# First mixer of a two-layer decoder trunk: narrow matmuls that add up in PSUM, an earlier softmax, and row sums from a token-major copy of x

## The chip, the cores and the metric

One Trainium2 chip; the kernel runs on 1 of its cores. The metric is device time in microseconds (us), the median of several runs; a profile is one execution seen by the hardware profiler.

## The reference

Two pre-norm residual layers on x of 256 tokens by 2048 channels, float32. The change touches the first layer's mixer only:

```python
h = rmsnorm(x, norm_mix[0])
u = h @ w_in                      # q, k, v (8 heads x 128), a, gate (1024 each)
q = partial_rope(q) * HEAD_DIM ** -0.5;  k = partial_rope(k)
y_a = dilated_attention(q, k, v)  # three causal windows, merged by their softmax sums
g = a * sigmoid(gate)
g = causal_dwconv(g, conv_w) + conv_b            # width 31
y_b = silu(layernorm(g))
x = x + concat([y_a, y_b]) @ w_out
```

After it come a gated FFN with a width-3 convolution, a second layer (forgetting attention and the same FFN), and a last norm.

## The kernel before, in words

Activations stand channel-major: `xT` holds 16 tiles of 128 channels by 256 tokens. Every operand of a large matmul is split in two parts, high and low: x into `xs` (L183 to L187: ACT makes the high part, DVE the low part), each piece of weights into `whi` (a cast on ACT, L95) and `wlo` (a subtraction on DVE, L96). `stream` (L79) loads weights through three raw buffers, all DMAs of it on SP's queue, splits them into four buffers of each part, and yields 2 row tiles at a time.

`panel_b` (L100) makes 512 output channels as four PSUM tiles (five exist). For each tile `m` and row tile `k` there are two matmuls: the high weights against both parts of x at once, 512 columns (L109), into the two halves of the tile, and the low weights against the high part of x, 256 columns (L110), into the left half. So the left half and the right half must be added when the tile is read: `whole` (L113) copies the right half on ACT and adds on DVE; `add_x` (L202) adds both halves to x on DVE. `panel_a` (L126), for v, has the tokens on the partitions and three matmuls of 512 columns.

The first mixer (L261 to L455) runs these panels in turn: four gate panels `ag0` to `ag3` (two tiles of a and two of gate each), `q0`, `q1`, `k0`, `k1`, the value panels `v0`, `v1`, the output projection of the attention half `oa0` to `oa3` (8 row tiles each), then of the convolution half `ob0` to `ob3`. The first norm's scale is applied after the projection, as `rb`. Its sum of squares comes from `square_x` (L189): ACT squares each tile of x, POOL adds (L195), four matmuls against ones (L179) sum over channels. `softmax_t` (L217) makes the scores of 4 heads (PE, L225), mask and maximum (DVE, L229), exponentials (ACT, L235), the scaling (ACT, L241), transposes (PE, L246) and copies back (ACT, L247); `weigh_v` (L250) multiplies with v. The convolution's 31 taps run on DVE and ACT beside all this, from a list that `fill_in` (L71) empties at a pace; after `oa1` the layer norm follows (L417): column sums (L425), the mean off (L432), squares, their sums (L434), a matmul (L179), the inverse root, its broadcast by a matmul (`bc_ln`, L169), then for each of 8 channel tiles a product (L437), Silu (L438), and the split into high (L439) and low (L440). `ob0` needs these.

A scheduler orders each engine's instructions by priorities and estimated times: `tc.high_priority(offset=n)` lets a block go ahead, `tc.issue_after` holds a DMA until another one is issued. The order is fixed at build time; each engine then works through its own list.

Of the kernel before, what the change touches and what calls it, by code (L numbers as in the profile page):

```python
# [41 lines left out]
def trunk(ctx, tc, a):  # L42
# [56 lines left out]

    def panel_b(src_of, x2, kts, name, order=(0, 1, 2, 3), dk=4):  # L100


        acc = {m: pacc.tile([P, 512], F32, tag="acc", name=f"acc_{name}_{m}") for m in order}
        for ks, hi, lo in stream(src_of, len(kts), P * len(order), name, dk):
            for m in order:
                ms = slice(m * P, (m + 1) * P)
                for j, k in enumerate(ks):
                    x = x2(kts[k])
                    PE.matmul(acc[m], hi[:, j, ms], x.rearrange("p a t -> p (a t)"), start=k == 0, stop=False)  # L109
                    PE.matmul(acc[m][:, :T], lo[:, j, ms], x[:, 0, :], start=False, stop=k == len(kts) - 1)  # L110
        return acc
# [51 lines left out]
    def along_free(r, name):  # L163
# [8 lines left out]
        return rb  # L172

    def rstd_from(parts, n, name):
# [5 lines left out]
        r = rsqrt_cols(ps[:, 0:2], 1.0 / n, name)  # L180
        return r, along_free(r, name)

# [6 lines left out]
    def square_x(kt, ssq, name):  # L189
        if kt == 0:  # L190
            S.activation(ssq, xT[:, kt, :], AF.Square)
        else:
            sq = wk.tile([P, T], F32, tag="sq", name=f"sq_{name}_{kt}")
            S.activation(sq, xT[:, kt, :], AF.Square)
            (G if name == "m0" else V).tensor_tensor(out=ssq, in0=ssq, in1=sq, op=ALU.add)  # L195

# [64 lines left out]
    with ExitStack() as ph:  # L261
# [121 lines left out]
        def qk_panel(c0, r, name):  # L383
            acc = panel_b(cols(w_in, c0 // 512), x2, list(range(KT)), name)
# [281 lines left out]
def _laid_out(inputs):  # L666
# [57 lines left out]
```

## Time and profile before

| | us |
|---|---|
| median of 3 runs | 2268.2 (2265.68 to 2268.28) |
| the profiled execution's own time | 2266.76 |
| its span, first to last instruction | 2265.0 |
| PE busy in the span | 2226.5 |
| DVE busy in the span | 1510.7 |
| ACT busy in the span | 1131.3 |

The profiled execution is 1.4 us under the median, and 1.8 us of it lie outside the span. Matmuls are pipelined and their ends are modelled, so PE's progress is read from the starts of its instructions and from its waits, not from its busy time.

### The profile page before, as it was taken

To read this page: it belongs to the slowest core of one execution; us is meant where nothing else is said; L and a number is where in the kernel's file an instruction comes from. 1 tells how busy PE (TensorE), PEld (TensorE's weight loads), DVE (VectorE), ACT (ScalarE), POOL (GpSimd) and SP (SyncE) were. 2 spreads that over 40 slices of the span, in tenths; PEclk is the share of its full clock that TensorE was granted. 3 is DMA by queue.
4 is the path that set the end of the run, shared out by engine and by line. 5 is a ranking of instruction groups with operands and counts; after the bars stand their busy time and mean duration, and the time that the engine had idled before them with its cause. 6 is when DMAs were issued, how large, how long until landed. Compare 5 with 4: busy or idle time off the path is not lost.

```text
span 2265.0 us, 30815 instructions
## 1 busy us (share of the span) xinstructions
PE 2226.5 (98%) x12142; PEld 1915.6 (85%) x12142; DVE 1510.7 (67%) x2307; ACT 1131.3 (50%) x1619; POOL 45.5 (2%) x77
## 2 busy tenths in 40 slices
PE   8999889999999999999999999999999999999997
PEld 7888778888888888888888888888888888888886
DVE  6999988776754576666655555666766644676644
ACT  6667655454443344444554444555444433444433
POOL 2000000000000000000010000000000000000001
PEclk9999899999999999999999999999999999999999
DMA  7554345555555545555545444555455555545453
GB/s 254 186 183 171 129 151 186 186 186 187 186 186 194 189 176 204 185 187 186 190 151 186 166 152 165 186 186 203 177 191 192 187 187 194 193 172 203 168 190 126
DMA packets 60225, 411.90 MB, mean 182 GB/s; under 512 B 7232, under 2 KB 7936, under 8 KB 11696
## 3 DMA queue, kind: packets, MB, share of 16 engines
q1 hardware_dynamic: 59328, 408.62, 50.7%
q8 instruction: 95, 1.56, 0.3%
q10 hardware_dynamic: 144, 1.05, 0.1%
q14 instruction: 50, 0.41, 0.1%
q0 software_dynamic: 608, 0.26, 0.0%
HBM read 407.75 MB, written 2.10 MB: 181 GB/s over the span
## 4 chain that ended last, share of the span: by engine, by line
PE 97%; DVE 1%; ACT 1%; DMA 0%; issue 0%; SPq 0%; ACTq 0%; DVEq 0%
PE acc_g L109 15%; PE acc_u L109 14%; PE acc_g L110 7%; PE acc_u L110 7%; PE acc_d L109 7%; PE acc_q L109 4%; PE acc_k L109 4%; PE acc_d L110 4%; PE acc_oc L109 3%; PE acc_ag L109 2%; PE acc_q L110 2%; PE acc_k L110 2%; PE acc_v L122 2%; PE acc_v L123 2%; PE acc_d L122 2%; PE acc_d L124 2%
## 5 line engine op out<-in xcount | busy, mean ns | idle before, releaser
L109 PE MATMUL acc_g<-xs,whi_g 128*128 128x512 f32 x1408 | 493.1, 397 | 0.0
L109 PE MATMUL acc_u<-xs,whi_u 128*128 128x512 f32 x1408 | 481.9, 395 | 0.0
L110 PE MATMUL acc_g<-xs,wlo_g 128*128 128x256 f32 x1408 | 388.8, 280 | 0.0
L110 PE MATMUL acc_u<-xs,wlo_u 128*128 128x256 f32 x1408 | 370.0, 279 | 0.0
L96 DVE TENSOR_TENSOR wlo_g<-raw_g,whi_g 128x1024 fp32r<-128x1024 f32 x176 | 215.1, 1223 | 166.2 <-ACT whi_g L95 166.2
L109 PEld LDWEIGHTS acc_g<-xs,whi_g 128*128 128x128 f32 x1408 | 262.6, 188 | 60.7
L95 ACT CAST whi_u<-raw_u 128x1024 fp32r<-128x1024 f32 x176 | 185.1, 1052 | 239.9 <-PE acc_u L109 122.0
L109 PEld LDWEIGHTS acc_u<-xs,whi_u 128*128 128x128 f32 x1408 | 260.1, 188 | 52.7
L96 DVE TENSOR_TENSOR wlo_u<-raw_u,whi_u 128x1024 fp32r<-128x1024 f32 x176 | 213.1, 1221 | 116.6 <-ACT whi_u L95 116.6
L95 ACT CAST whi_g<-raw_g 128x1024 fp32r<-128x1024 f32 x176 | 184.9, 1051 | 198.1 <-PE acc_u L109 91.3
L96 DVE TENSOR_TENSOR wlo_d<-raw_d,whi_d 128x1024 fp32r<-128x1024 f32 x136 | 166.5, 1224 | 161.5 <-ACT whi_d L95 161.3
L110 PEld LDWEIGHTS acc_u<-xs,wlo_u 128*128 128x128 f32 x1408 | 265.0, 188 | 9.0
L110 PEld LDWEIGHTS acc_g<-xs,wlo_g 128*128 128x128 f32 x1408 | 265.6, 189 | 3.0 <-DVE wlo_g L96 0.2
L95 ACT CAST whi_d<-raw_d 128x1024 fp32r<-128x1024 f32 x136 | 143.0, 1051 | 207.2 <-PE acc_d L109 118.9
L109 PE MATMUL acc_d<-hp,whi_d 128*128 128x512 f32 x704 | 245.2, 394 | 0.0
L110 PE MATMUL acc_d<-hp,wlo_d 128*128 128x256 f32 x704 | 194.4, 283 | 0.0
L109 PEld LDWEIGHTS acc_d<-hp,whi_d 128*128 128x128 f32 x704 | 131.3, 188 | 28.8
L110 PEld LDWEIGHTS acc_d<-hp,wlo_d 128*128 128x128 f32 x704 | 132.3, 188 | 1.9
L109 PE MATMUL acc_q<-xs,whi_q 128*128 128x512 f32 x384 | 133.8, 396 | 0.0
L109 PE MATMUL acc_k<-xs,whi_k 128*128 128x512 f32 x384 | 131.7, 394 | 0.0
L110 PE MATMUL acc_q<-xs,wlo_q 128*128 128x256 f32 x384 | 104.5, 282 | 0.0
L110 PE MATMUL acc_k<-xs,wlo_k 128*128 128x256 f32 x384 | 102.0, 279 | 0.0
(296 smaller groups left out, 3858.4 us busy)
## 6 DMA issues: line engine op xcount, KB each, us to landing
raw_g<-in_ffn_w_up SPq DMA_DIRECT2D x88, 1024.0 KB, 4.8
raw_u<-in_ffn_w_up SPq DMA_DIRECT2D x88, 1024.0 KB, 4.8
raw_d<-in_ffn_w_down SPq DMA_DIRECT2D x68, 1024.0 KB, 4.8
raw_q<-in_od_w_in SPq DMA_DIRECT2D x16, 1024.0 KB, 4.8
raw_k<-in_od_w_in SPq DMA_DIRECT2D x16, 1024.0 KB, 4.8
raw_v<-in_od_w_in SPq DMA_DIRECT2D x16, 1024.0 KB, 4.8
raw_oc<-in_od_w_out SPq DMA_DIRECT2D x16, 1024.0 KB, 4.8
raw_e<-in_ffn_w_down SPq DMA_DIRECT2D x16, 1024.0 KB, 4.7
```

What stands on the lines that cost most here:

```text
L95: S.copy(hi, rv[:, h:h + half, :])
L96: last = V.tensor_tensor(out=lo, in0=rv[:, h:h + half, :], in1=hi.bitcast(F32), op=ALU.subtract)
L109: PE.matmul(acc[m], hi[:, j, ms], x.rearrange("p a t -> p (a t)"), start=k == 0, stop=False)
L110: PE.matmul(acc[m][:, :T], lo[:, j, ms], x[:, 0, :], start=False, stop=k == len(kts) - 1)
L122: PE.matmul(o, xh, hi, start=first, stop=False)
L123: PE.matmul(o, xh, lo, start=False, stop=False)
L124: PE.matmul(o, xl, hi, start=False, stop=last)
```

## The change

It does five things in the first mixer, and nothing elsewhere.

1. `panel_b` gets `wide=False` for `ag`, `q`, `k` and `oa`: the 512-column matmul becomes two of 256 columns with the same weights, one for each part of x, both into the left half of the PSUM tile. All products then add up in PSUM.
2. Readers of these tiles take one half: `whole` goes, the q and k panels multiply by the norm's scale straight from PSUM, `add_x` makes one addition instead of two, and `ag_glu` is rewritten.
3. The first norm's sums: x is loaded a second time, token-major, in four pieces of 128 by 1024; ACT squares each with an accumulated row sum, DVE adds two sums per token. The sixteen squares, POOL's additions and four matmuls go.
4. `softmax_t` of the first mixer is traced with `high_priority(offset=200)`.
5. A host-side copy of x in the inputs (`x_tok`), and a function split in two (`rstd_of`).

```diff
-    def panel_b(src_of, x2, kts, name, order=(0, 1, 2, 3), dk=4):
+    def panel_b(src_of, x2, kts, name, order=(0, 1, 2, 3), dk=4, wide=True):
...
-                    PE.matmul(acc[m], hi[:, j, ms], x.rearrange("p a t -> p (a t)"), start=k == 0, stop=False)
+                    if wide:
+                        PE.matmul(acc[m], hi[:, j, ms], x.rearrange("p a t -> p (a t)"), start=k == 0, stop=False)
+                    else:
+                        PE.matmul(acc[m][:, :T], hi[:, j, ms], x[:, 0, :], start=k == 0, stop=False)
+                        PE.matmul(acc[m][:, :T], hi[:, j, ms], x[:, 1, :], start=False, stop=False)
...
-    def add_x(acc, i, then=None):
+    def add_x(acc, i, then=None, wide=True):
...
-            V.tensor_tensor(out=x, in0=acc[m][:, T:], in1=x, op=ALU.add)
+            if wide:
+                V.tensor_tensor(out=x, in0=acc[m][:, T:], in1=x, op=ALU.add)
             V.tensor_tensor(out=x, in0=acc[m][:, :T], in1=x, op=ALU.add)
...
-                for kt in range(c, c + n):
-                    square_x(kt, ssq0, "m0")
...
             for j in range(2):
-                whole(sg[:, j, :], acc[2 + j], f"g{i}{j}")
+                V.tensor_tensor(out=sg[:, j, :], in0=acc[2 + j][:, :T], in1=rb, op=ALU.mult)
+            S.activation(sg, sg, AF.Sigmoid)
+            V.tensor_tensor(out=sg, in0=sg, in1=rb.unsqueeze(1).broadcast_to([P, 2, T]), op=ALU.mult)
             for j in range(2):
-                whole(ab[:, j, :], acc[j], f"a{i}{j}")
-            V.tensor_tensor(out=sg, in0=sg, in1=rb2, op=ALU.mult)
-            S.activation(sg, sg, AF.Sigmoid)
-            V.tensor_tensor(out=sg, in0=sg, in1=rb2, op=ALU.mult)
-            V.tensor_tensor(out=ab, in0=ab, in1=sg, op=ALU.mult)
+                V.tensor_tensor(out=glu[:, 2 * i + j, KW - 1:], in0=acc[j][:, :T], in1=sg[:, j, :], op=ALU.mult)
...
+        with tc.high_priority(offset=400):
+            for i in range(4):
+                t, h = divmod(i, 2)
+                xtok = x0.tile([P, 1024], F32, name=f"xtok{i}", tag="xtok", bufs=2)
+                with tc.issue_after(loads[4].ins):
+                    nc.sync.dma_start(out=xtok, in_=a["x_tok"][t * P:(t + 1) * P, 1024 * h:1024 * (h + 1)])
+                S.activation(xtok, xtok, AF.Square, accum_out=sq0[:, i:i + 1])
+            V.reduce_sum(out=ss0, in_=sq0.rearrange("p (t h) -> p t h", t=2), axis=AX.X)
...
             for m in range(4):
-                whole(full[:, m, :], acc[m], f"{name}{m}")
-            V.tensor_tensor(out=full, in0=full, in1=r.unsqueeze(1).broadcast_to([P, 4, T]), op=ALU.mult)
+                V.tensor_tensor(out=full[:, m, :], in0=acc[m][:, :T], in1=r, op=ALU.mult)
...
-            pts.append(softmax_t(mx, qf[hg], kf, mask, f"e{hg}", act_scale=True))
+            with tc.high_priority(offset=200):
+                pts.append(softmax_t(mx, qf[hg], kf, mask, f"e{hg}", act_scale=True))
```

From the first matmul of `ob0` on, PE's and DVE's lists are the same in both kernels. Ahead of it the scheduler places many things anew. Three places follow. The lines of the changed kernel are its own: L113 and L114 are the two narrow matmuls, L115 the low weights' (L110 before), L255 the transposes (L246), L348 the new loads, L282 the loads of x (L274).

SP's queue in the first gate panel, before (L86 loads weights, L336 and L337 constants):

```order
L86 DMA raw_ag_6_192<-in_ev_w_in 128x1024
L86 DMA raw_ag_8_224<-in_ev_w_in 128x1024
L86 DMA raw_ag_10_257<-in_ev_w_in 128x1024
L86 DMA raw_ag_12_290<-in_ev_w_in 128x1024
L86 DMA raw_ag_14_322<-in_ev_w_in 128x1024
L336 DMA cst<-in_c_ident 128x130
L337 DMA cw<-in_ev_conv_w 128x248
L86 DMA raw_ag_0_399<-in_ev_w_in 128x2048
L86 DMA raw_ag_4_448<-in_ev_w_in 128x2048
```

and now:

```order
L86 DMA raw_ag_6_199<-in_ev_w_in 128x1024
L86 DMA raw_ag_8_233<-in_ev_w_in 128x1024
L348 DMA xtok_375<-in_x_tok 128x1024
L348 DMA xtok_378<-in_x_tok 128x1024
L86 DMA raw_ag_10_268<-in_ev_w_in 128x1024
L86 DMA raw_ag_12_303<-in_ev_w_in 128x1024
L86 DMA raw_ag_14_337<-in_ev_w_in 128x1024
L348 DMA xtok_381<-in_x_tok 128x1024
L341 DMA cst<-in_c_ident 128x130
L342 DMA cw<-in_ev_conv_w 128x248
L348 DMA xtok_384<-in_x_tok 128x1024
L86 DMA raw_ag_0_418<-in_ev_w_in 128x2048
```

Two of the new loads stand ahead of the panel's sixth piece of weights, two ahead of the next panel's first.

PE at the end of the second value panel, before: the transposes of the second softmax (`tp_e_2121` and on) stand behind the panel's last matmuls.

```order
L122 MATMUL acc_v_1_2341<-whi_v_14_2487,xs 128x512
L123 MATMUL acc_v_1_2341<-wlo_v_14_2488,xs 128x512
L124 MATMUL acc_v_1_2341<-whi_v_14_2487,xs 128x512
L246 MATMUL tp_e_2121<-cst,pt_e_2085 128x128 x3
L246 MATMUL tp_e_2128<-cst,pt_e_2086 128x128 x3
L246 MATMUL tp_e_2135<-cst,pt_e_2087 128x128 x3
L246 MATMUL tp_e_2142<-cst,pt_e_2088 128x128 x3
L253 MATMUL y_e_2320<-pt_e_1789,vt_2317 128x256
L254 MATMUL y_e_2320<-pt_e_1789,vt_2317 128x128
L253 MATMUL y_e_2325<-pt_e_1790,vt_2317 128x256
L254 MATMUL y_e_2325<-pt_e_1790,vt_2317 128x128
```

Now nine of its twelve transposes stand within the panel's piece 10 of 14, with 30 matmuls of the panel behind them; the scores (L234) stand in `v0`.

```order
L128 MATMUL acc_v_1_2742<-wlo_v_10_2847,xs 128x512
L129 MATMUL acc_v_1_2742<-whi_v_10_2846,xs 128x512
L127 MATMUL acc_v_1_2742<-whi_v_10_2846,xs 128x512
L255 MATMUL tp_e_2522<-cst,pt_e_2486 128x128
L128 MATMUL acc_v_1_2742<-wlo_v_10_2847,xs 128x512
L255 MATMUL tp_e_2522<-cst,pt_e_2486 128x128 x2
L255 MATMUL tp_e_2529<-cst,pt_e_2487 128x128 x3
L255 MATMUL tp_e_2536<-cst,pt_e_2488 128x128 x3
L129 MATMUL acc_v_1_2742<-whi_v_10_2846,xs 128x512
L127 MATMUL acc_v_0_2741<-whi_v_12_2870,xs 128x512
```

PE around the broadcast of the layer norm (`bc_ln`), before: in piece 2 of `oa3`, with 10 pairs of matmuls between it and `ob0`.

```order
L110 MATMUL acc_oa_2_2937<-y_1087,wlo_oa_2_2962 128x256
L109 MATMUL acc_oa_2_2937<-y_1087,whi_oa_2_2961 128x512
L110 MATMUL acc_oa_2_2937<-y_1087,wlo_oa_2_2962 128x256
L169 MATMUL bc_ln<-dg_ln,ones 128x256
L109 MATMUL acc_oa_3_2938<-y_1087,whi_oa_2_2961 128x512
L110 MATMUL acc_oa_3_2938<-y_1087,wlo_oa_2_2962 128x256
L109 MATMUL acc_oa_3_2938<-y_1087,whi_oa_2_2961 128x512
L110 MATMUL acc_oa_3_2938<-y_1087,wlo_oa_2_2962 128x256
L109 MATMUL acc_oa_2_2937<-y_1087,whi_oa_4_2983 128x512
```

Now it stands in piece 4 of `oa3`, with 44 narrow matmuls between it and `ob0`.

```order
L113 MATMUL acc_oa_0_3420<-y_1268,whi_oa_4_3484 128x256
L114 MATMUL acc_oa_0_3420<-y_1268,whi_oa_4_3484 128x256
L115 MATMUL acc_oa_0_3420<-y_1268,wlo_oa_4_3485 128x256
L113 MATMUL acc_oa_0_3420<-y_1268,whi_oa_4_3484 128x256
L174 MATMUL bc_ln<-dg_ln,ones 128x256
L114 MATMUL acc_oa_0_3420<-y_1268,whi_oa_4_3484 128x256
L115 MATMUL acc_oa_0_3420<-y_1268,wlo_oa_4_3485 128x256
L113 MATMUL acc_oa_1_3421<-y_1268,whi_oa_4_3484 128x256
L114 MATMUL acc_oa_1_3421<-y_1268,whi_oa_4_3484 128x256
L115 MATMUL acc_oa_1_3421<-y_1268,wlo_oa_4_3485 128x256
```

## Rows read from the trace of the kernel before

**Rows 1.** The profile's page: the busy time, share and number of instructions of each engine, and the shares of the chain that ended last.

```profile
PE 2226.5 (98%) x12142; PEld 1915.6 (85%) x12142; DVE 1510.7 (67%) x2307; ACT 1131.3 (50%) x1619; POOL 45.5 (2%) x77
...
PE 97%; DVE 1%; ACT 1%; DMA 0%; issue 0%; SPq 0%; ACTq 0%; DVEq 0%
```

**Rows 2.** The view of waits for PE over the whole span, the four longest: who was waited for, us in total, times, longest in us.

```profile
PE acc_ag L109 <- ACT whi_ag L95: 8.2, 2, 7.1
PE tp_e L246 <- ACT pt_e L241: 6.3, 1, 6.3
PE acc_ob L109 <- DVE y L440: 4.2, 2, 3.9
...
PE acc_oa L110 <- DVE wlo_oa L96: 2.0, 3, 1.2
```

**Rows 3.** The timeline of PE in the first gate panel: start in us, us, engine, line, operation, tiles, shape, count, and in brackets the idle time before it and who ended it.

```profile
19.14 1.19 PE L109 MATMUL acc_ag<-xs,whi_ag 128*128 128x512 f32 x4 [1.06 <-ACT whi_ag L95]
21.95 0.39 PE L110 MATMUL acc_ag<-xs,wlo_ag 128*128 128x256 f32 x1 [1.61 <-DVE wlo_ag L96]
```

**Rows 4.** The timeline of ACT in the same stretch, same columns.

```profile
14.25 1.70 ACT L185 ACTIVATE xs<-xT,vcol 128x256 fp32r<-128x256 f32 x4
...
18.06 1.03 ACT L95 CAST whi_ag<-raw_ag 128x1024 fp32r<-128x1024 f32 x1
```

**Rows 5.** The timeline of DVE in the same stretch, same columns.

```profile
5.13 0.88 DVE L186 SCALAR_TENSOR_TENSOR xs<-xT,vcol,xs 128x256 fp32r<-128x256 f32 x2 [4.13 <-ACT xs L185]
...
15.55 5.21 DVE L186 SCALAR_TENSOR_TENSOR xs<-xT,vcol,xs 128x256 fp32r<-128x256 f32 x8
20.68 4.56 DVE L96 TENSOR_TENSOR wlo_ag<-raw_ag,whi_ag 128x1024 fp32r<-128x1024 f32 x3
...
30.22 1.23 DVE L96 TENSOR_TENSOR wlo_ag<-raw_ag,whi_ag 128x1024 fp32r<-128x1024 f32 x1 [2.32 <-ACT whi_ag L95]
```

**Rows 6.** The view of stretches: from and to in us, their length, then busy us and number of instructions of PE, PEld, DVE, ACT and POOL, the granted TensorE clock (1.00 is 2.4 GHz, 0.50 is 1.2 GHz), the DMA engines' share, GB/s.

```profile
22.50:25.80 3.30, 3.30 (x13) 2.91 (x12) 2.73 (x2) 1.04 (x3) 3.16 (x2) 0.50 0.70 231
...
247.80:261.30 13.50, 8.40 (x29) 6.68 (x30) 13.08 (x30) 12.14 (x39) 0.00 (x0) 0.50 0.22 78
...
319.50:322.80 3.30, 3.05 (x10) 2.24 (x9) 2.90 (x8) 2.68 (x9) 0.00 (x0) 0.50 0.72 243
```

**Rows 7.** The timeline of PE from the second value panel to the output projection, columns as in rows 3.

```profile
225.21 1.03 PE L246 MATMUL tp_e<-cst,pt_e 128*128 128x128 f32 x8
226.00 0.48 PE L123 MATMUL acc_v<-wlo_v,xs 128*128 128x512 f32 x1
...
238.91 1.47 PE L225 MATMUL s_e<-k,q 128*128 128x128 f32 x8
...
251.73 2.47 PE L246 MATMUL tp_e<-cst,pt_e 128*128 128x128 f32 x9 [6.32 <-ACT pt_e L241]
...
261.04 0.64 PE L109 MATMUL acc_oa<-y,whi_oa 128*128 128x512 f32 x1
...
262.70 0.59 PE L253 MATMUL y_e<-pt_e,vt 128*128 128x256 f32 x2
...
263.27 0.48 PE L109 MATMUL acc_oa<-y,whi_oa 128*128 128x512 f32 x1
```

**Rows 8.** The timeline of PE at the end of the layer norm, same columns.

```profile
310.17 0.59 PE L169 MATMUL bc_ln<-dg_ln,ones 128*128 128x256 f32 x2
...
314.01 0.28 PE L110 MATMUL acc_oa<-y,wlo_oa 128*128 128x256 f32 x1
318.23 0.47 PE L109 MATMUL acc_ob<-y,whi_ob 128*128 128x512 f32 x1 [3.93 <-DVE y L440]
```

**Rows 9.** The timeline of DVE at the end of the layer norm, same columns.

```profile
312.05 2.77 DVE L437 TENSOR_TENSOR cacc<-cacc,rb_ln 128x256 f32<-128x256 f32 x8
...
317.67 0.41 DVE L440 TENSOR_TENSOR y<-cacc,y 128x256 fp32r<-128x256 f32 x1
```

**Rows 10.** The view of stretches (columns as in rows 6) for the whole stretch in which the convolution's taps run.

```profile
33.00:284.00 251.00, 243.51 (x1317) 209.55 (x1317) 231.41 (x440) 168.94 (x305) 0.00 (x0) 0.97 0.49 175
```

**Rows 11.** The timeline of PE in the third gate panel, columns as in rows 3.

```profile
95.05 0.39 PE L109 MATMUL acc_ag<-xs,whi_ag 128*128 128x512 f32 x1
95.27 0.40 PE L110 MATMUL acc_ag<-xs,wlo_ag 128*128 128x256 f32 x2
95.51 0.40 PE L109 MATMUL acc_ag<-xs,whi_ag 128*128 128x512 f32 x1
...
96.81 1.08 PE L109 MATMUL acc_ag<-xs,whi_ag 128*128 128x512 f32 x4
97.73 0.28 PE L110 MATMUL acc_ag<-xs,wlo_ag 128*128 128x256 f32 x1
```

**Rows 12.** The timeline of PEld, the weight loads, in the same panel.

```profile
95.05 0.41 PEld L110 LDWEIGHTS acc_ag<-xs,wlo_ag 128*128 128x128 f32 x2
95.39 0.19 PEld L109 LDWEIGHTS acc_ag<-xs,whi_ag 128*128 128x128 f32 x1
```

**Rows 13.** The view of groups of instructions by line and shape, 0 to 360 us: names, shapes, count, busy us and mean ns of one, idle us before them.

```profile
L205 DVE TENSOR_TENSOR xT<-acc_oa,xT 128x256 f32<-128x256 f32 x16 | 6.3, 417 | 1.3 <-PE acc_oa L110 1.2
...
L306 DVE TENSOR_TENSOR sg<-sg,rb_n 128x512 f32<-128x512 f32 x4 | 2.7, 680 | 0.0
...
L389 DVE TENSOR_TENSOR q<-q,rq 128x1024 f32<-128x1024 f32 x2 | 2.4, 1216 | 0.0
```

More of the change, by code (lines that the diff above doesn't have):

```diff
@@ L172, in along_free, with rstd_of @@
         return rb
+    def rstd_of(sums, n, name):
+        r = rsqrt_cols(sums, 1.0 / n, name)
+        return r, along_free(r, name)
     def rstd_from(parts, n, name):
@@ L179, in rstd_from @@
                 PE.matmul(ps[:, t:t + 1], ssq[:, t * P:(t + 1) * P], ones[:, 0:1], start=i == 0, stop=i == len(parts) - 1)
-        r = rsqrt_cols(ps[:, 0:2], 1.0 / n, name)
-        return r, along_free(r, name)
+        return rstd_of(ps[:, 0:2], n, name)
     def split_x(kt, gcol):
@@ L194, in square_x @@
             S.activation(sq, xT[:, kt, :], AF.Square)
-            (G if name == "m0" else V).tensor_tensor(out=ssq, in0=ssq, in1=sq, op=ALU.add)
+            V.tensor_tensor(out=ssq, in0=ssq, in1=sq, op=ALU.add)
     def finish_x(kt, gcol, ssq, name):
@@ L270, in trunk @@
         x0 = x0_scope.enter_context(tc.tile_pool(name="x0", bufs=1))
-        ssq0 = new_ssq("m0")
         def load_x(k0, k1):
@@ L282, in ag_gemm @@
             if i > 0:
-                return panel_b(srcs, x2, list(range(KT)), f"ag{i}", order=(2, 3, 0, 1))
+                return panel_b(srcs, x2, list(range(KT)), f"ag{i}", order=(2, 3, 0, 1), wide=False)
             def first(c, n):
@@ L291, in first @@
                         split_x(kt, kt)
-                for kt in range(c, c + n):
-                    square_x(kt, ssq0, "m0")
                 return srcs(c, n)
-            return panel_b(first, x2, list(range(KT)), "ag0", order=(2, 3, 0, 1), dk=2)
+            return panel_b(first, x2, list(range(KT)), "ag0", order=(2, 3, 0, 1), dk=2, wide=False)
         def ag_glu(acc, i):
             sg = x0.tile([P, 2, T], F32, tag="sg", name=f"sg_{i}", bufs=2)
-            rb2 = rb.unsqueeze(1).broadcast_to([P, 2, T])
-            ab = glu[:, 2 * i:2 * i + 2, KW - 1:]
             for j in range(2):
-                whole(sg[:, j, :], acc[2 + j], f"g{i}{j}")
+                V.tensor_tensor(out=sg[:, j, :], in0=acc[2 + j][:, :T], in1=rb, op=ALU.mult)
+            S.activation(sg, sg, AF.Sigmoid)
+            V.tensor_tensor(out=sg, in0=sg, in1=rb.unsqueeze(1).broadcast_to([P, 2, T]), op=ALU.mult)
             for j in range(2):
-                whole(ab[:, j, :], acc[j], f"a{i}{j}")
-            V.tensor_tensor(out=sg, in0=sg, in1=rb2, op=ALU.mult)
-            S.activation(sg, sg, AF.Sigmoid)
-            V.tensor_tensor(out=sg, in0=sg, in1=rb2, op=ALU.mult)
-            V.tensor_tensor(out=ab, in0=ab, in1=sg, op=ALU.mult)
+                V.tensor_tensor(out=glu[:, 2 * i + j, KW - 1:], in0=acc[j][:, :T], in1=sg[:, j, :], op=ALU.mult)
         def conv_tap(c, j):
@@ L334, in trunk @@
         acc0 = ag_gemm(0)
+        ss0 = x0.tile([P, 2], F32, name="ss0")
+        sq0 = x0.tile([P, 4], F32, name="sq0")
         with tc.issue_after(loads[-1].ins):
@@ L337, in trunk @@
             nc.sync.dma_start(out=cw, in_=a["ev_conv_w"])
+        with tc.high_priority(offset=400):
[6 more added lines that the diff above has]
+            V.reduce_sum(out=ss0, in_=sq0.rearrange("p (t h) -> p t h", t=2), axis=AX.X)
         with tc.high_priority(offset=300):
-            rcol, rb = rstd_from([ssq0], D, "n0")
+            rcol, rb = rstd_of(ss0, D, "n0")
             rq = mx.tile([P, T], F32, name="rq0")
@@ L383, in qk_panel @@
         def qk_panel(c0, r, name):
-            acc = panel_b(cols(w_in, c0 // 512), x2, list(range(KT)), name)
+            acc = panel_b(cols(w_in, c0 // 512), x2, list(range(KT)), name, wide=False)
             full = mx.tile([P, 4, T], F32, tag=name[0], name=name, bufs=2)
@@ L444, in trunk @@
         for i in range(4):
-            acc = panel_b(cols(w_out, i), lambda k: y2[:, k, :, :], list(range(8)), f"oa{i}")
-            add_x(acc, i)
+            acc = panel_b(cols(w_out, i), lambda k: y2[:, k, :, :], list(range(8)), f"oa{i}", wide=False)
+            add_x(acc, i, wide=False)
             if i == 1:
@@ L671, in _laid_out @@
     given["vecs"] = np.concatenate(vecs, axis=1)
+    given["x_tok"] = given["x"][0]
     given["x"] = given["x"][0].T.reshape(KT, P, T).transpose(1, 0, 2)
```

## The prediction

> **What bounds the kernel now.** I read the page first: PE's work makes 97% of the chain that ended last, so time is won only where PE waits or runs slowly, and lost wherever PE gets more work [rows 1]. The view of waits then says where it waits: all the long ones that the change can reach lie in the first mixer [rows 2]. Three places, read in the timelines:
>
> First, the first gate panel. PE waits 1.06 us for the cast of weights and then 1.61 us for their low part, and its low matmul starts only at 21.95 us [rows 3]. Behind it stand ACT, where eight splits of x and some squares precede that cast, which starts at 18.06 us [rows 4], and DVE, where eight splits of x take 5.21 us, 0.65 us each, while two took 0.88 us (0.44 each) at the start; the low parts of weights take 1.52 us each there and 1.23 us later [rows 5]. The slow ones coincide with POOL, which is busy 3.16 of 3.30 us from 22.5 us on. In that stretch the granted clock is 0.50, the lower level of 1.2 GHz [rows 6].
>
> Second, the second softmax. Its transposes come behind all matmuls of the value panels, PE waits 6.32 us for ACT's scaling until 251.73 us, and the output projection starts only at 261.04 us; so 15.6 us lie between the last value matmul's end (251.73 - 6.32 = 245.41) and the first of `oa` [rows 7]. From 247.8 to 261.3 us the granted clock is 0.50 [rows 6].
>
> Third, the layer norm's end: `ob0` starts at 318.23 us after 3.93 us of waiting [rows 8] for the low part of the first channel tile, which DVE delivers at 317.67 + 0.41 = 318.08 us, 7.9 us after the broadcast matmul at 310.17 us [rows 8, 9]. The clock falls to 0.50 again just after, for 3.3 us [rows 6]. DVE is nearly full all this time: 231.4 of 251 us [rows 10].
>
> **The change, part by part.** The sum is made against the profiled execution's 2266.8 us, 1.4 us under the median of the runs shown.
>
> *Narrow matmuls.* Eight panels of 64 pairs and four of 32 give 640 pairs; each loses a wide matmul and gets two narrow ones. The trace has both widths in a row: four wide ones go from 96.81 to 97.73 us, 0.230 us each, and two narrow ones, each with its own weights, from 95.27 to 95.51 us [rows 11]. From 95.05 to 97.73 us stand 8 wide and 7 narrow: with 0.2325 us for a wide one, a narrow one takes 0.117 to 0.118. So a pair costs 0.0045 us more, 640 of them **+2.9 us**. Bounds: 0, since the columns are the same and half of 0.230 is the least for a narrow one, and +0.010 each, the difference as two decimals read (0.24 against 0.23), 6.4 us. The weight loads double for the high part; a load's record lasts 0.19 us, longer than a narrow matmul, but a third load starts 0.34 us after the first of two whose records reach 0.41 us, so records overlap [rows 12]. I take that side because two narrow matmuls in a row show no gap; a long run of them is not in the trace.
>
> *Start.* Squares leave ACT, POOL's additions leave altogether. DVE's splits then cost 0.44 instead of 0.65 us: begun at about 15.2, eight end near 18.7, and the low part, at 1.23 us, at 19.9 instead of 22.2 us. PE's low matmul comes at 20.0 instead of 21.95: 1.95 us. If so little waiting is left, the stretch at half clock, 3.3 us for 1.65 us of work, need not come. Together **-3.6 us**, bounds 0 and -5. What is added lies beside PE: 4 loads of 0.5 MB, 4 squares with row sums on ACT. The first two loads stand ahead of weights that PE needs only at 24 us; SP's third and fourth wait for ACT's first squares and hold up the next panel's weights behind them, needed some 13 us later.
>
> *Softmax.* Of the 15.6 us, work is 12 transposes (8 take 0.79 us at full clock) 1.2 us, and four heads of weighted v, 0.57 us each, 2.3 us [rows 7]: 3.5 us. Now the last scores come ahead of `v1`, and the transposes 70 value matmuls of 512 columns later, 16.1 us at 0.230 us each. Before, the chain from the last scores (238.91 + 1.47 = 240.38 us) to the transposes at 251.73 took 11.3 us [rows 7]. So PE should find them ready: **-12.1 us**; bounds -9, if 3 us of new waits appear, and -12.5.
>
> *Less work for DVE and ACT.* Per q or k panel DVE saves one product of 1.22 us, per gate panel two of 0.68 us, and eight additions of 0.42 us in `oa0` and `oa1` [rows 13]: 4.9 + 5.4 + 3.3 = 13.6 us before the layer norm. PE isn't waiting for that work, so by itself it counts zero; it decides whether the layer norm follows when PE comes earlier. DVE's 231.4 us less 13.6 in a stretch that shrinks by 251 - 13 = 238 us leave 20 us idle, as now, so it should.
>
> *Layer norm.* 44 narrow matmuls of 0.118, 5.2 us, now stand between the broadcast and `ob0`, before it was 3.8 us (310.17 to 314.01 and one narrow). With the same 7.9 us behind the broadcast the wait falls from 3.93 to about 2.6 us. The 2.0 us of waits for low weights in `oa` [rows 2] fall away with DVE's relief, and 0.5 us of slow restarts: **-3.8 us**, bounds 0 and -8. The half-clock stretch after it may stay or go: **-0.8 us**, half of its 1.65.
>
> Sum: 2.9 - 3.6 - 12.1 - 3.8 - 0.8 = -17.4; 2266.8 - 17.4 = 2249.4, and 1.4 up to the median: **2250.8, say 2251 us**. From `ob0` on nothing moves.
>
> **The rivals.**
>
> *DVE holds the layer norm.* If DVE stays the bound up to `ob0`, PE's gain at the softmax turns into a wait before `ob0`, and the mixer ends earlier only by DVE's 13.6 us: 2268.2 - 13.6 = 2254.6 us. For it: 92% of DVE's time is busy. Against: 20 us of slack. 17%.
>
> *The start gains nothing*: the new loads share the queue with the first weights, PE still waits and the clock falls. 2251 + 3.6 = 2254.6 us. 8%.
>
> *PSUM held longer.* In a gate panel the two tiles of a were emptied at once; now they wait for the sigmoid and its product. The next panel's fourth tile needs one of them. The order leaves some 64 narrow matmuls, 7.5 us, for two products, two casts, a table load, the sigmoid and two products, some 6 us. If it is 2 us late in each of four panels: 2259 us. 9%.
>
> *Weight loads in the open: slower.* If a run of narrow matmuls can't hide every load, each of the 640 extra loads adds up to its recorded 0.19 us: +120 us, 2371 us. It decides the sign once the extra load costs over 0.03 us (17.4 + 2.9 over 640). Against: the pairs of narrow matmuls without a gap [rows 11]. 4%. The Trainium skill, TensorE: Matmul & The Clock Gate, section "Part 3: Packing small matmuls", says that a weight load overlaps a running matmul only when it goes to another group of rows; all loads here fill all rows, so by that rule this rival would be the forecast. The trace disagrees: 0.117 us per narrow matmul leaves no room for a load of 0.19 us in the open.
>
> **How the numbers follow.** My forecast, 62%. Its own bounds add up to 2241 at the best (0 for the narrow matmuls, -5, -12.5, -8, -1.65) and some 2258 with the narrow ones at 6.4 and the softmax at -9. With the three rivals at 2255 to 2259 and a part of their bounds I give 2240 to 2261. What a measurement here can tell from no change is about 0.2%, 4.5 us: faster means below 2263.7. Forecast and three rivals lie there, 96%; 4 of these 96 I give to several small losses that together end within 0.2%. So faster 0.92, same 0.04, slower 0.04, the last rival.
>
> **What would show it.** Right: PE's wait for the scaled softmax gone, `oa` starting near 248 us, no stretch at 0.50 there; narrow matmuls 0.117 to 0.119 us apart in long runs; `ob0` near 301 us after a wait of 2 to 3 us. Wrong: starts of narrow matmuls 0.15 us apart or more; a wait of 8 us or more before `ob0`; waits of PE for DVE's reading of a gate tile at the start of panels; the first panel's end still near 37 us.

## The result and the profile after

Median 2251.45 us (2249.79 to 2253.19, 4 runs) against 2267.8 us (2265.68 to 2268.28): ratio 0.9927, 95% interval 0.9914 to 0.9939 (the kernel before has one run more here than in its table). The forecast was 2251 us. The size came out; not every reason did, as the experiments show.

The page of the profile after, as [rows 1]:

```profile
PE 2225.6 (99%) x12778; PEld 1946.7 (86%) x12778; DVE 1493.7 (66%) x2280; ACT 1120.5 (50%) x1579; POOL 29.6 (1%) x62
...
PE 97%; DMA 1%; DVE 1%; ACT 0%; SPq 0%; issue 0%; ACTq 0%; DVEq 0%
```

PE's busy time is the same with 636 more instructions; the share rose because the span is 14.1 us shorter. DVE has 17 us less work.

The view of waits for PE, 0 to 360 us, as [rows 2]:

```profile
PE acc_ag L113 <- ACT whi_ag L95: 6.7, 1, 6.7
PE bc_n L174 <- DVE dg_n L172: 1.9, 1, 1.9
PE acc_ob L111 <- DVE y L453: 1.4, 1, 1.4
PE acc_ag L115 <- DVE wlo_ag L96: 0.4, 2, 0.2
```

The 6.3 us for the scaled softmax are gone, as are `oa`'s 2.0 us for low weights; the layer norm's wait fell from 3.9 to 1.4. A wait of 1.9 us is new, for the first norm's broadcast `bc_n`.

Starts of PE's first matmuls, in us:

| | before | after | shift |
|---|---|---|---|
| first matmul | 7.09 | 6.67 | -0.4 |
| last of the first gate panel | 37.02 | 32.42 | -4.6 |
| second value panel | 219.42 | 225.82 | +6.4 |
| `oa` | 261.04 | 250.86 | -10.2 |
| `ob` | 318.23 | 303.33 | -14.9 |
| FFN | 365.52 | 348.79 | -16.7 |

To the last matmul the profiled execution loses 2.4 us of this again in code that is the same; another execution of the same lists (e1 below) keeps 16.3 us. So the mixer is read at the FFN's start.

**Start.** Timeline of PE around the end of the first gate panel (answers to [rows 3]):

```profile
32.42 0.28 PE L115 MATMUL acc_ag<-xs,wlo_ag 128*128 128x256 f32 x1
34.63 0.70 PE L174 MATMUL bc_n<-dg_n,ones 128*128 128x256 f32 x2 [1.94 <-DVE dg_n L172]
34.98 0.47 PE L113 MATMUL acc_ag<-xs,whi_ag 128*128 128x256 f32 x1
35.29 0.28 PE L114 MATMUL acc_ag<-xs,whi_ag 128*128 128x256 f32 x1
35.77 0.39 PE L115 MATMUL acc_ag<-xs,wlo_ag 128*128 128x256 f32 x1 [0.20 <-DVE wlo_ag L96]
```

and of ACT, the squares of the third and fourth token-major load:

```profile
28.56 1.06 ACT L349 ACTIVATE xtok<-xtok 128x1024 f32<-128x1024 f32 x1 [2.27 <-DMA xtok<-in_x_tok]
...
30.41 1.06 ACT L349 ACTIVATE xtok<-xtok 128x1024 f32<-128x1024 f32 x1 [0.70 <-DMA xtok<-in_x_tok]
```

The panel's last matmul comes 4.6 us earlier. Then PE stands before `bc_n`: ACT waited for the loads, and the chain from the fourth square to `dg_n` takes the rest.

**Softmax.** ACT's scaling of the second softmax, then PE's transposes, the end of the value panels and the first of `oa` (answers to [rows 7]):

```profile
236.76 2.88 ACT L250 ACTIVATE pt_e<-pt_e,den_e 128x128 f32<-128x128 f32 x8
```

```profile
241.70 0.27 PE L255 MATMUL tp_e<-cst,pt_e 128*128 128x128 f32 x1
...
242.04 1.03 PE L255 MATMUL tp_e<-cst,pt_e 128*128 128x128 f32 x8
...
247.50 0.49 PE L255 MATMUL tp_e<-cst,pt_e 128*128 128x128 f32 x3
...
250.06 0.39 PE L129 MATMUL acc_v<-whi_v,xs 128*128 128x512 f32 x1
250.29 0.59 PE L262 MATMUL y_e<-pt_e,vt 128*128 128x256 f32 x2
...
250.86 0.72 PE L113 MATMUL acc_oa<-y,whi_oa 128*128 128x256 f32 x4
```

The scaling begins 4.9 us before PE turns to its first tile; nine transposes are covered by value matmuls, of which 25 come behind them (the section on the change counts 30). The stretch from the second value panel's first matmul to `oa` shrinks from 41.6 to 25.0 us.

Stretches (columns as in [rows 6]): a piece of q, the place of the half clock at the softmax, and the one behind the layer norm:

```profile
110.00:140.00 30.00, 30.00 (x253) 30.00 (x252) 26.73 (x47) 18.83 (x30) 0.00 (x0) 1.00 0.52 181
...
247.00:261.00 14.00, 14.00 (x102) 13.22 (x101) 13.02 (x26) 9.63 (x20) 0.00 (x0) 1.00 0.40 149
303.50:307.00 3.50, 3.50 (x21) 3.05 (x22) 2.49 (x6) 3.50 (x10) 0.00 (x0) 1.00 0.00 0
```

Both half-clock stretches are at 1.00 now. In the first row the weight loads are busy for the whole 30 us, which comes back below.

**Layer norm.** PE, then DVE (answers to [rows 8, 9]):

```profile
296.16 0.59 PE L174 MATMUL bc_ln<-dg_ln,ones 128*128 128x256 f32 x2
...
301.67 0.28 PE L115 MATMUL acc_oa<-y,wlo_oa 128*128 128x256 f32 x1
303.33 0.50 PE L111 MATMUL acc_ob<-y,whi_ob 128*128 128x512 f32 x1 [1.38 <-DVE y L453]
```

```profile
302.86 0.42 DVE L453 TENSOR_TENSOR y<-cacc,y 128x256 fp32r<-128x256 f32 x1
```

From the broadcast to the first low part it is 302.86 + 0.42 - 296.16 = 7.1 us, 0.8 less than before.

**Narrow matmuls**, a run of them in q (answers to [rows 11]):

```profile
119.80 0.28 PE L113 MATMUL acc_q<-xs,whi_q 128*128 128x256 f32 x1
119.92 0.28 PE L114 MATMUL acc_q<-xs,whi_q 128*128 128x256 f32 x1
120.04 0.28 PE L113 MATMUL acc_q<-xs,whi_q 128*128 128x256 f32 x1
```

0.120 us each, steadily, in gate, q and k panels; in `oa` the mean of undisturbed ones is 0.118. Three take 0.360 us against 0.3505 for a wide and a narrow one before.

### The profile page after: what moved, and what is told of

The parts are those of the page before. It is cut to its first block, busy times and chain, and to the rows that moved or that the text cites. A ratio compares the mean times of both kernels' runs of the same rounds, so it can differ in the third digit from the quotient of the medians.

```text
span 2250.9 us, 31982 instructions
## 1 busy us (share of the span) xinstructions
PE 2225.6 (99%) x12778; PEld 1946.7 (86%) x12778; DVE 1493.7 (66%) x2280; ACT 1120.5 (50%) x1579; POOL 29.6 (1%) x62
## 4 chain that ended last, share of the span: by engine, by line
PE 97%; DMA 1%; DVE 1%; ACT 0%; SPq 0%; issue 0%; ACTq 0%; DVEq 0%
PE acc_g L111 15%; PE acc_u L111 14%; PE acc_g L115 7%; PE acc_u L115 7%; PE acc_d L111 7%; PE acc_d L115 4%; PE acc_oc L111 3%; PE acc_k L111 3%; PE acc_q L111 3%; PE acc_q L115 2%; PE acc_k L115 2%; PE acc_v L127 2%; PE acc_v L128 2%; PE acc_d L127 2%; PE acc_d L129 2%; PE acc_v L129 2%
## 5 line engine op out<-in xcount | busy, mean ns | idle before, releaser
L115 PE MATMUL acc_g<-xs,wlo_g 128*128 128x256 f32 x1408 | 389.5, 281 | 0.0
L115 PE MATMUL acc_u<-xs,wlo_u 128*128 128x256 f32 x1408 | 370.7, 280 | 0.0
L115 PEld LDWEIGHTS acc_u<-xs,wlo_u 128*128 128x128 f32 x1408 | 265.3, 188 | 9.0
L115 PEld LDWEIGHTS acc_g<-xs,wlo_g 128*128 128x128 f32 x1408 | 266.0, 189 | 3.0 <-DVE wlo_g L96 0.2
L115 PE MATMUL acc_d<-hp,wlo_d 128*128 128x256 f32 x704 | 194.8, 283 | 0.0
L115 PEld LDWEIGHTS acc_d<-hp,wlo_d 128*128 128x128 f32 x704 | 132.6, 188 | 1.9
L115 PE MATMUL acc_q<-xs,wlo_q 128*128 128x256 f32 x384 | 106.2, 284 | 0.0
L115 PE MATMUL acc_k<-xs,wlo_k 128*128 128x256 f32 x384 | 106.0, 281 | 0.0
L96 DVE TENSOR_TENSOR wlo_v<-raw_v,whi_v 128x1024 fp32r<-128x1024 f32 x48 | 58.7, 1223 | 48.2 <-ACT whi_v L95 47.6
L111 PE MATMUL acc_q<-xs,whi_q 128*128 128x512 f32 x256 | 90.6, 396 | 0.0
```

The costliest lines, as they stand in the source:

```text
L96: last = V.tensor_tensor(out=lo, in0=rv[:, h:h + half, :], in1=hi.bitcast(F32), op=ALU.subtract)
```

## The experiments

Ratios are to the kernel before, with 95% intervals; `oa`, `ob` and FFN are PE's first matmuls there in the trace.

| | us | ratio | oa | ob | FFN |
|---|---|---|---|---|---|
| e1 without priority | 2250.1 | 0.992 (0.9906 to 0.9934) | 250.8 | 303.3 | 348.7 |
| e2 narrow and readers only | 2254.4 | 0.9938 (0.9925 to 0.995) | 254.8 | 307.3 | 352.7 |
| e3 sums only | 2270.3 | 1.001 (1.0001 to 1.0019) | 262.0 | 320.6 | 368.0 |
| e4 old readers in q, k | 2256.8 | 0.9949 (0.9936 to 0.9961) | 256.7 | 309.2 | 354.7 |
| e5 short readers, wide | 2250.0 | 0.9919 (0.9906 to 0.9933) | 247.9 | 300.9 | 347.9 |
| e6 four buffers | 2249.7 | 0.992 (0.9906 to 0.9934) | 249.7 | 302.1 | 347.6 |
| e8 `oa` wide | 2259.0 | 0.9961 (0.9948 to 0.9973) | 251.9 | 309.0 | 357.1 |
| e9 fewer taps early | 2278.8 | 1.0048 (1.0034 to 1.0062) | 251.8 | 329.5 | 377.5 |
| e10 gate panels wide | 2252.6 | 0.9934 (0.9922 to 0.9947) | 250.1 | 303.0 | 348.4 |

**e1.** The changed kernel, and

```diff
-            with tc.high_priority(offset=200):
-                pts.append(softmax_t(mx, qf[hg], kf, mask, f"e{hg}", act_scale=True))
+            pts.append(softmax_t(mx, qf[hg], kf, mask, f"e{hg}", act_scale=True))
```

> The changed kernel without its fourth part: the first mixer's softmax is traced at its ordinary priority. The scheduler then gives every engine the same list as in the changed kernel. Theory (the softmax came ahead because the readers of the q, k and gate tiles got shorter, not because of the priority): 2251.4 us, the same as the changed kernel, PE without a wait for the scaled softmax. Rival (the priority carries the softmax's gain): some 12 us more, 2263 us, with a wait of about 6 us before the transposes.

The changed kernel's time, and its start of the FFN within 0.1 us; in the two traces PE, DVE, ACT and POOL work through the same lists. PE has no wait for the softmax. So the fourth part does nothing here.

**e2.** The kernel before, with the change's new `panel_b`, `add_x`, `ag_glu` and reader of `qk_panel`, and their calls:

```diff
-                return panel_b(srcs, x2, list(range(KT)), f"ag{i}", order=(2, 3, 0, 1))
+                return panel_b(srcs, x2, list(range(KT)), f"ag{i}", order=(2, 3, 0, 1), wide=False)
...
-            acc = panel_b(cols(w_in, c0 // 512), x2, list(range(KT)), name)
+            acc = panel_b(cols(w_in, c0 // 512), x2, list(range(KT)), name, wide=False)
...
-            add_x(acc, i)
+            add_x(acc, i, wide=False)
```

> The kernel before with the first two parts alone: narrow matmuls in ag, q, k and oa and the readers of one half; sums of squares as before, no priority. Theory: everything but the start's 2.4 us is here: 2253.8 us (2252 to 2256), output projection within 3 us of the changed kernel's 250.9 us in the trace. Rival (the new sums carry more than the start, because they take work off ACT and POOL): over 2258 us.

As the theory had it. Its waits for PE:

```profile
PE acc_ag L113 <- ACT whi_ag L95: 9.0, 3, 7.3
PE acc_ag L115 <- DVE wlo_ag L96: 1.9, 2, 1.6
PE acc_ob L111 <- DVE y L445: 1.4, 1, 1.4
```

The waits of the start are close to those of before; everything from the softmax on is that of the changed kernel, 3.9 us later (4.0 against e1). So with the other parts the new sums are worth some 4 us, and the narrow panels with their readers the rest. Some of the 4 us stands already in the first matmul, which starts at 7.27 us here and at 6.83 in e1; over all runs it lies between 6.65 and 7.27.

**e3.** The kernel before, with the third part's diff alone:

```diff
-                for kt in range(c, c + n):
-                    square_x(kt, ssq0, "m0")
...
+                    nc.sync.dma_start(out=xtok, in_=a["x_tok"][t * P:(t + 1) * P, 1024 * h:1024 * (h + 1)])
+                S.activation(xtok, xtok, AF.Square, accum_out=sq0[:, i:i + 1])
+            V.reduce_sum(out=ss0, in_=sq0.rearrange("p (t h) -> p t h", t=2), axis=AX.X)
...
-            rcol, rb = rstd_from([ssq0], D, "n0")
+            rcol, rb = rstd_of(ss0, D, "n0")
```

> The kernel before with the third part alone: row sums from the token-major load, wide matmuls. Theory: only the start moves, by -2.4 us as in the changed kernel, and the wait of 6 us for the scaled softmax stays: 2265.4 us (2264 to 2267). Rival (the start's gain is larger, and the new wait at the norm's broadcast comes from the faster narrow panel): 2263 us or less. Second rival (2 MB more on the queue cost what the sums give): 2267.8 us.

None of the three: alone the new sums make it slower by 0.1%. Waits for PE, 0 to 360 us; the granted clock behind the first gate panel; PE's last scores and ACT's scaling; and that scaling in the kernel before:

```profile
PE tp_e L249 <- ACT pt_e L244: 9.7, 1, 9.7
PE acc_ag L109 <- ACT whi_ag L95: 9.0, 2, 6.9
PE acc_ob L109 <- DVE y L451: 4.0, 1, 4.0
```

```profile
36.00:39.00 3.00, 3.00 (x11) 2.61 (x11) 3.00 (x6) 2.98 (x3) 0.00 (x0) 0.50 0.47 101
```

```profile
243.25 0.82 PE L228 MATMUL s_e<-k,q 128*128 128x128 f32 x4
...
253.30 2.86 ACT L244 ACTIVATE pt_e<-pt_e,den_e 128x128 f32<-128x128 f32 x8
```

```profile
251.29 2.87 ACT L241 ACTIVATE pt_e<-pt_e,den_e 128x128 f32<-128x128 f32 x8
```

The first panel ends 5 us earlier, but the next one's weights are late by 2.1 us (9.0 - 6.9), and the half clock takes some 1.6 us there (an estimate: what is left of the 3.8 us lost between the first panel's end and the second value panel once the waits are taken off). So PE comes to the second value panel 1.4 us earlier than before, and that is spent waiting for the scaled softmax, 9.7 instead of 6.3 us. The other 2 us of that wait are new: the order is another one, the last scores start at 243.25 us, behind the value panel (before, at 238.91, within it), and ACT's scaling begins at 253.30 instead of 251.29 us. A gain at the start counts only where the softmax doesn't hold PE behind it, and here the softmax moved as well.

**e4.** The changed kernel, and in q and k

```diff
-                V.tensor_tensor(out=full[:, m, :], in0=acc[m][:, :T], in1=r, op=ALU.mult)
+                half = wk.tile([P, T], F32, tag="half", name=f"half_{name}{m}", bufs=3)
+                S.copy(half, acc[m][:, :T])
+                V.tensor_tensor(out=full[:, m, :], in0=acc[m][:, :T], in1=half, op=ALU.add)
+            V.tensor_tensor(out=full, in0=full, in1=r.unsqueeze(1).broadcast_to([P, 4, T]), op=ALU.mult)
```

> The changed kernel with the long readers back in q and k alone: a copy of the half by ACT, an addition and one product over 1024 columns by DVE (the copy takes the same half again, so q and k come out doubled); the matmuls stay narrow, the priority stays. Per panel DVE gets four additions and loses three short products. Theory: the softmax's transposes fall behind the value panels again, the wait and the clock's fall come back, +10 to +13 us: 2262 to 2264 us. Rival (the narrow matmuls or the priority bring the softmax forward): 2251 to 2253 us.

Between the two, and nearer to the theory in kind. ACT's scaling and its copies of transposed tiles out of PSUM (L256), then PE's transposes, then the clock:

```profile
246.94 2.87 ACT L250 ACTIVATE pt_e<-pt_e,den_e 128x128 f32<-128x128 f32 x8
...
252.60 1.19 ACT L256 COPY pt_e<-tp_e 128x384 f32<-128x384 f32 x3
```

```profile
247.68 1.93 PE L255 MATMUL tp_e<-cst,pt_e 128*128 128x128 f32 x9
253.11 0.90 PE L255 MATMUL tp_e<-cst,pt_e 128*128 128x128 f32 x3 [3.50 <-ACT pt_e L256]
```

```profile
252.50:255.50 3.00, 2.39 (x8) 2.13 (x9) 2.82 (x5) 3.00 (x9) 0.00 (x0) 0.50 0.27 57
```

The transposes stand behind the value panels again, and the scaling begins 10.2 us later than in the changed kernel (246.94 against 236.76 us). But the wait that the theory names does not come back: PE turns to the first transpose at 247.68 us, when its tile is scaled. What PE waits for, 3.5 us, is ACT's copy of a transposed tile, which stands behind other work of ACT. The clock falls at that wait, and `oa` starts 5.8 us later. So short readers in q and k bring the softmax forward, with matmuls that are narrow in both. Two things are not separated: the readers take work off ACT (the copies) and off DVE at once, and the fixed order moves with them.

**e5.** The changed kernel, and in the four calls of `panel_b` for ag, q, k and `oa` (the one of `oa` shown)

```diff
-            acc = panel_b(cols(w_out, i), lambda k: y2[:, k, :, :], list(range(8)), f"oa{i}", wide=False)
+            acc = panel_b(cols(w_out, i), lambda k: y2[:, k, :, :], list(range(8)), f"oa{i}", wide=True)
```

> The changed kernel with wide matmuls again in ag, q, k and oa, and the short readers kept: they read the left half only, so the product of the high weights with the low part of x is left out of the results. Theory (the readers' shorter work on DVE and ACT brings the softmax forward; the narrow matmuls themselves only cost, 512 pairs by 0.0095 and 128 by 0.0035 us): 5.3 us less than the changed kernel, 2245 to 2247 us, no wait for the scaled softmax. Rival (DVE and ACT then hold the softmax or the layer norm, so that PE's saved 5.3 us come back as waits of 4 to 6 us more): 2250 to 2252 us.

The rival's number. Waits for PE, and the clock behind `ob`'s start:

```profile
PE acc_ob L111 <- DVE y L453: 3.0, 1, 3.0
PE bc_n L174 <- DVE dg_n L172: 2.4, 1, 2.4
```

```profile
301.00:305.00 4.00, 4.00 (x15) 3.42 (x16) 2.46 (x5) 3.90 (x10) 0.00 (x0) 0.60 0.00 0
```

PE saves 5.3 us of matmuls by the expectation's estimate and is 3.0 us ahead of the changed kernel at `oa` and 2.4 at `ob`; it waits longer before `bc_n` (2.4 against 1.9 us) and before `ob` (3.0 against 1.4), and behind both waits the clock falls (0.50 from 36 to 39 us, and the row above), where the changed kernel's stays at 1.00. At the FFN 0.9 us are left. So the softmax gain needs no narrow matmul, only short readers; and most of the narrow matmuls' own cost is time that PE would here have waited or run at half clock.

**e6.** The changed kernel, and

```diff
-                xtok = x0.tile([P, 1024], F32, name=f"xtok{i}", tag="xtok", bufs=2)
-                with tc.issue_after(loads[4].ins):
+                xtok = x0.tile([P, 1024], F32, name=f"xtok{i}", tag="xtok", bufs=4)
+                with tc.issue_after(loads[4 if i < 2 else 7].ins):
```

> The changed kernel with four buffers instead of two for the token-major loads, the third and fourth issued right behind the first panel's last weights: they no longer wait for ACT's squares of the first two. Theory (the wait of 1.9 us before the norm's broadcast and the 1.3 us after it are the third load's wait on its buffer, with the queue idle meanwhile): the broadcast comes 2 to 3 us earlier, 2248 to 2249.5 us, the rest of the order unchanged. Rival (the queue's 2 MB more are the limit, whatever their order): 2250.5 to 2251.5 us, the wait stays or moves to the next panel's weights.

PE at the broadcast:

```profile
33.31 0.70 PE L174 MATMUL bc_n<-dg_n,ones 128*128 128x256 f32 x2 [0.77 <-DVE dg_n L172]
...
34.56 0.38 PE L115 MATMUL acc_ag<-xs,wlo_ag 128*128 128x256 f32 x1 [0.32 <-DVE wlo_ag L96]
```

Half of the theory came true: PE is 1.3 us earlier at `bc_n`, its wait there falls from 1.9 to 0.8 us, and 1.2 us are left at the FFN (1.1 against e1). By the median, 2249.7 us, it can't be told from e1. By its trace it is the best of the versions that compute the whole result, by little.

**e7.** The changed kernel, run once, and in q and k

```diff
-                    PE.matmul(acc[m][:, :T], lo[:, j, ms], x[:, 0, :], start=False, stop=k == len(kts) - 1)
+                    n = P if name in ("q0", "q1", "k0", "k1") else T
+                    PE.matmul(acc[m][:, :n], lo[:, j, ms], x[:, 0, :n], start=False, stop=k == len(kts) - 1)
```

> The changed kernel with the low matmul of the q and k panels over 128 instead of 256 columns (the low weights' part of the second 128 tokens is left out). It measures what sets 0.120 us per narrow matmul there. If columns set it: a low matmul takes 0.067 us, the three of a pair 0.307 us. If the load of the weights sets it: the low matmul still takes 0.110 to 0.120 us, the three 0.35 to 0.36 us. Forecast: the second, since the load engine is busy for 100% of these panels. Its total time is not compared, the softmax's order is another one.

The same piece of q as above:

```profile
110.00:140.00 30.00, 30.00 (x259) 30.00 (x258) 26.84 (x46) 18.79 (x28) 0.00 (x0) 1.00 0.55 196
```

A sixth of the columns is gone and the pace goes from 0.120 to 0.116 us per matmul only (first to last start of the row's matmuls). After a matmul of 128 columns the next start follows in 0.06 us, and the one after that takes 0.165, longer than the 0.120 of the changed kernel for as many columns. So neither the columns nor a fixed time per matmul set the pace; the weight loads, busy throughout, are what is left. Their own starts lie 0.108 to 0.126 us apart.

**e8.** The changed kernel, `oa` wide with two additions per tile:

```diff
-            acc = panel_b(cols(w_out, i), lambda k: y2[:, k, :, :], list(range(8)), f"oa{i}", wide=False)
-            add_x(acc, i, wide=False)
+            acc = panel_b(cols(w_out, i), lambda k: y2[:, k, :, :], list(range(8)), f"oa{i}")
+            add_x(acc, i)
```

> The changed kernel with wide matmuls and two additions per tile in oa alone. The order then has the layer norm's broadcast right before ob0, behind all of oa, where the changed kernel has 44 narrow matmuls between them. Theory (DVE's additions delay the layer norm, whose end of 7 to 8 us behind the broadcast is then in the open): a wait before ob0 of 6 to 8 us instead of 1.4 us, 2256 to 2258 us. Rival (DVE has room, oa's part is worth little): 2250 to 2252 us.

The theory's direction: the time is 1 us beyond its range, the wait just under it. The wait; the clock behind it; and the clock behind the first gate panel:

```profile
PE acc_ob L111 <- DVE y L453: 5.7, 1, 5.7
```

```profile
309.00:313.00 4.00, 4.00 (x13) 3.42 (x14) 2.27 (x7) 3.68 (x10) 0.00 (x0) 0.50 0.15 61
```

```profile
36.00:38.00 2.00, 2.00 (x11) 2.00 (x11) 2.00 (x5) 1.98 (x3) 0.00 (x0) 0.50 0.56 90
```

`ob` starts 5.7 us later, and 2.7 us more are lost until the FFN, most of them at half clock, which the expectation forgot. Its lists up to `oa` are those of the changed kernel. Yet behind a wait of 1.7 us before `bc_n` its clock falls to 0.50, and the changed kernel's stays at 1.00 behind 1.9 us; so that stretch differs from one execution to the next.

**e9.** The kernel before, and one line:

```diff
-P_AG, P_Q, P_K, P_V, P_O = 2.4, 2.6, 2.6, 2.4, 3.4
+P_AG, P_Q, P_K, P_V, P_O = 1.6, 2.0, 2.0, 2.4, 4.4
```

> The kernel before with another pace of the convolution's taps: fewer beside the gate, q and k panels, more beside oa (1.6, 2.0, 2.0, 2.4, 4.4 instead of 2.4, 2.6, 2.6, 2.4, 3.4). No work is taken away; matmuls stay wide, readers long. The order then has the second softmax's scores ahead of v0's and v1's ends and most of its transposes within v1, as in the changed kernel. Theory (DVE's work ahead of the softmax decides where it comes, and DVE's total decides where the layer norm ends): the wait for the scaled softmax is gone, oa starts 8 to 12 us earlier, and the time comes back as a wait of 10 to 14 us before ob0, which starts between 316 and 322 us as before: 2264 to 2270 us. Rival (an early softmax is worth its 12 us by itself): 2255 to 2258 us.

Waits for PE:

```profile
PE mu L426 <- DVE csum L425: 11.2, 1, 11.2
...
PE ss_ln L179 <- DVE csq L434: 6.0, 2, 4.8
PE acc_ob L109 <- DVE y L440: 3.7, 1, 3.7
PE bc_ln L169 <- DVE dg_ln L167: 2.0, 1, 2.0
```

The softmax's wait is gone and `oa` starts 9.3 us earlier, with all matmuls wide and all readers long. Then PE waits 23 us for DVE's layer norm, at a clock of 0.50 for most of that time, and `ob` starts 11 us later than before. An early softmax bought by moving DVE's work is given back with interest; the interest (the layer norm's steps come one after the other, with nothing of `oa` left beside them) was not expected.

**e10.** The changed kernel with the gate panels as before:

```diff
-                return panel_b(srcs, x2, list(range(KT)), f"ag{i}", order=(2, 3, 0, 1), wide=False)
+                return panel_b(srcs, x2, list(range(KT)), f"ag{i}", order=(2, 3, 0, 1))
...
-                V.tensor_tensor(out=sg[:, j, :], in0=acc[2 + j][:, :T], in1=rb, op=ALU.mult)
+                whole(sg[:, j, :], acc[2 + j], f"g{i}{j}")
...
-                V.tensor_tensor(out=glu[:, 2 * i + j, KW - 1:], in0=acc[j][:, :T], in1=sg[:, j, :], op=ALU.mult)
+                whole(ab[:, j, :], acc[j], f"a{i}{j}")
```

> The changed kernel with wide matmuls and the old readers (copies by ACT, additions and longer products by DVE) in the gate panels alone; q, k and oa as changed. PE has 2.4 us less, DVE 5.4 us more. Theory (DVE's work decides): the transposes of the second softmax stand behind v1 again, part of the wait comes back, and the end of the layer norm is later too: 2254 to 2258 us. Rival (PE's time decides, the gate panels' readers had cover): 2249 us.

The theory said 2254 to 2258 and the rival 2249; it measured 2252.6, and its runs (2249.3 to 2256.3) reach both. In the trace the FFN starts 0.4 us before the changed kernel's. The transposes do stand behind the value panels, and a wait is back, as in e4 for ACT's copy of a transposed tile and not for the scaling:

```profile
PE tp_e L255 <- ACT pt_e L256: 2.8, 1, 2.8
```

but PE's shorter panels pay for it. The gate panels' share of the change, narrow matmuls and short readers together, is worth nothing that can be seen: by this trace, what the readers give, the matmuls take.

## Why the prediction was right, step by step

**Narrow matmuls, +2.9: mis-sized.** 512 pairs by 0.0095 and 128 by some 0.0035 us make 5.3 us, inside the bounds of 0 and 6.4. The step that failed is "two narrow matmuls in a row show no gap": in a long run each takes 0.120 us, not 0.1175. These 5.3 us come from undisturbed runs of matmuls and are rather low: from the first panel's end to `v0`, 448 of the 640 pairs cost some 5.1 us more than before (an estimate from the two traces, with PE's waits and the scores that moved there taken off). And they don't add to the sum as written: e5 takes them away and gets 0.9 us.

**Start, -3.6: right in sum, wrong inside.** e2 against e1 gives 4.0 us, of which 0.4 stand in the first matmul. The panel ends 4.6 us earlier, and the half clock is gone as forecast, though e8 shows that it can come back with the same lists; but "The first two loads stand ahead of weights that PE needs only at 24 us" looked at weights and not at who waits for the sums. The wait for `bc_n` was not on the list.

**Softmax, -12.1: right in size, unnamed in cause.** The prediction took the new place from the order and didn't ask which edit made it. It isn't the priority (e1); it is the readers of q and k (e4), of whose relief the prediction wrote: "by itself it counts zero". The wait of 6.3 us is gone, the half clock of 13.5 us too, and the stretch from `v1` to `oa` is 16.6 us shorter, of which some 3.3 us are the scores and transposes that now stand ahead of it (2.2 and 1.1 us of PE), and 0.6 us weighted values that now stand behind it. That leaves 12.7 us; the bound was 12.5.

**Less work for DVE and ACT, 0: the step that failed as reasoning.** With the long readers back, q and k cost 5.9 us at the FFN (e4). With long readers and wide matmuls back, `oa` costs 8.3 us (e8) and the gate panels gain 0.4 (e10), where the wide matmuls alone would gain some 0.4 and 2.4 us (the pairs' prices above and the expectation's estimate). So the relief is not zero: it is most in `oa` and in q and k, and some 2 us in the gate panels by one trace. DVE was no spectator with 20 us idle: with fewer taps beside the early panels the softmax comes forward and the layer norm falls back, and PE's waits are the difference (e9). ACT's copies went with the same edits, so its share is not shown. The first rival named this and was right about the mechanism; it didn't come true, since the wait before `ob` fell to 1.4 us.

**Layer norm, -3.8:** from `oa` to `ob` 57.2 us became 52.5, 4.7 less; the wait is 1.4 us where 2.6 were forecast. **Half clock, -0.8:** from `ob` to the FFN 47.3 us became 45.5, 1.8 less, the whole of it. e5 and e8 show the other side: before `ob`, behind a wait of 3.0 or 5.7 us it falls again, behind 1.4 it doesn't in this trace.

**The other rivals.** The changed kernel's trace has no wait of PE on DVE's reading of a gate tile (e2's has one, of 0.2 us): "PSUM held longer" fell. "Weight loads in the open" fell, too: the pair costs 0.0095 us, a third of the 0.03 from which it decides. But it was closer than 4% makes it sound: the loads are the pace (e7). The Trainium skill's rule (TensorE: Matmul & The Clock Gate, "Part 3: Packing small matmuls") that a load overlaps only a matmul on other rows doesn't hold here: loads with records of 0.19 us follow one another each 0.12 us beside matmuls on all rows. The same section of the Trainium skill also lets a load go ahead into a background weight buffer; whether that is the way here, no run shows.

Sum up to the FFN: -17.4 forecast, -16.7 measured. That they are so close is in part luck: `oa` comes at 250.9 us and not near 248, since the narrow matmuls and the wait before `bc_n` cost more, and from `oa` to the FFN 6.5 us are won where 4.6 were forecast.

## What to carry to other kernels

Where an engine off the chain is nine tenths full, don't cost its relief at zero: ask at which hand-over PE meets it, and test that with the relief alone and with the relief taken back panel by panel. When a list of instructions moves, find out which edit moved it before crediting the one that says so. A gain at the start is only as good as the next place where PE waits anyway: the same edit was +2.2 us alone and -4 us beside the others.

## What the runs showed of the hardware

Weight loads of 128 by 128 follow one another at 0.116 us on average at full clock with a third of the matmuls at 128 columns (e7), and at 0.120 with all at 256. So at 256 columns the loads already are about the pace, and narrower matmuls gain little: a sixth of the columns less gave 3%. Long runs of 256-column matmuls were steady at 0.120 us in gate, q and k and 0.118 in `oa`, for which the runs give no reason. With the same lists at the start the clock fell to 0.50 in one execution (e8, from 36 to 38 us, behind a wait of 1.7 us) and stayed at 1.00 in another (the changed kernel, behind 1.9 us).
